# Column sums of the adaLN accumulators: matmuls with a column of ones, or transposes and row sums

## The chip, the cores and the metric

The kernel runs on one core of a Trainium2 chip. The metric is the device time of one execution in microseconds (us). Before the change the median of three runs is 1148.0 us (1146.42 to 1149.65).

## The reference

The program is a trunk of two layers over x (256 x 2048, f32) with a conditioning vector c of 2048 values. What the change touches is the modulation:

```python
cond = jax.nn.silu(c)
for i in range(DEPTH):
    mod = cond @ ada_w[i] + ada_b[i]
    shift, scale, gate = jnp.split(mod, 3, axis=-1)
    h = rms_norm(x, pre_g[i]) * (1 + scale[:, None, :]) + shift[:, None, :]
    ...
    y = sgu_mixer(h, ...) if i == 0 else mla_mixer(h, ...)
    x = x + gate[:, None, :] * rms_norm(y, post_g[i])
```

`ada_w[i]` is 2048 x 6144 f32, 50 MB per layer, and it is multiplied by a single vector. The mixer of layer 0 (SGU) projects h to 3 x 4096 columns (`u`, `v`, `z`), normalizes and mixes `v` along the sequence, multiplies, and projects back from 4096 to 2048. The mixer of layer 1 (MLA) projects h to 3072 columns (two latents, a rotary key, a gate `z`), expands the latents to 16 heads, attends, and projects back.

## The kernel before, in words

All large products run on PE with f32r operands that were split into a high and a low part; a product of two such numbers takes three matmuls. The weights come in **granules**: one load of 256 rows x 512 columns (512 KB) on SP's queue, a cast to the high part on ACT (line 113), and the difference to the low part on DVE (line 114). One granule feeds 12 matmuls of 128x512, since the 256 tokens are two blocks, each with two k-tiles and three products.

The class `Stream` sets the order of this work. `load` appends a transfer, `weights` a transfer with its stage of casting and subtracting, `hook` any other stage. When the matmuls of a granule are about to be written into the program, `get` runs stages until the one that is `AHEAD` + 1 = 5 granules further on is made (hooks on the way are run as they come), and `step` keeps the transfers `RAW_BUFS` = 6 loads ahead of the stages. The engines' programs are written in that order and each runs its own in order.

The modulation is too small for PE at full width, so it is done on DVE. `ada_items` makes one item per k-tile of 128 rows: a load into the same ring of raw buffers, and a hook that adds raw * silu(c)[k] to an accumulator `acc` of 128 x 1024 (line 294 for the first, 296 for the others). After 16 k-tiles the accumulator holds, for 1024 outputs, 128 partial sums each, one on each partition, which must be summed across the partitions, and the sums must lie on partitions as columns. `ada_sums` (line 305) does both with PE: for each 128 columns of the accumulator one matmul with a column of ones, eight for an accumulator of 1024, into one auxiliary bank (`aux_bank`, a ring of four PSUM banks that transposes and the SGU's mixing use as well). Its readers on DVE follow in the same hook: `ada_put` (lines 316 to 320) adds the bias to the shift and makes `amul`, `fin` of `ada_gate` (lines 347 and 349) makes `gcol`.

There are eight accumulators of 1024 from the middle of layer 0 on: two for layer 0's gate (`ada_gate(0)`, tiles `acc_gate`, `pgate`), four for layer 1's shift and scale (`ada_range(1, ...)`, tiles `acc_ada`, `pada`), two for layer 1's gate (`ada_gate(1)`). Layer 0's own shift and scale come before, in smaller ranges, and go through the same `ada_sums`.

The items are dealt out evenly among the granules by `spread`. The constants say how many: `E1` items of layer 0's gate go with the last part of the `u` and `v` projection, `E2` items with the `z` projection (`piz`), the rest with layer 0's output projection (`po`); of `gate1`, `G1` items go with layer 1's input projection (`pm`), the rest with the last output projection (`pp`). A gate half is 17 items, 16 accumulations and `fin`.

In layer 1 the two latents are normalized and turned while `pm_3` runs: `turn_latent` is called four times, a granule apart, with tiles `cqp`, `cqp`, `ckp`, `ckp`. Each takes an auxiliary bank, turns into it, and is read in the next granule by ACT (line 1058) and in the one after by DVE (line 1064), where the bank becomes free. `spread_gate` later turns `gcol` and broadcasts it along the rows through DRAM.

Of the kernel before, what the change touches and what calls it, by code (L numbers as in the profile page):

```python
# [12 lines left out]
AX = mybir.AxisListType  # L13
PSUM = bass.MemoryType.PSUM

P = 128
# [25 lines left out]
MUL = 3  # L42
AHEAD0 = 2
RAMP = 15
G1 = 23
E1 = 23
E2 = 32
LAG = 6
LAG1 = 7
PRE = 4  # L50
# [90 lines left out]
def spread(main, extra):  # L141

    if not main:
        return
    done = 0
    for i, m in enumerate(main):
        m()
        want = -(-len(extra) * (i + 1) // len(main))
        while done < want:
            extra[done]()  # L150
            done += 1
# [3 lines left out]
def tile_trunk(  # L155
# [7 lines left out]
    nc = tc.nc  # L163
    x = x[0]
    out = out[0]
# [10 lines left out]
    ST = Stream(nc, wp)  # L176
# [4 lines left out]
    def small(name, n):  # L181
        return sp.tile([P, n], F32, tag="sm", name=name, bufs=16)
# [4 lines left out]
    def aux_bank(name):  # L187
        return pa.tile([P, 512], F32, tag="ax", name=name)
# [15 lines left out]
    ident = const.tile([P, P], F32, name="ident")  # L204
# [72 lines left out]
    def ada_items(name, src, width, state):  # L277

        nk = 1024 // width
        todo = []  # L280
        for k in range(KD):
            def add(k=k):
                if k % nk == 0:
                    state["box"] = ST.raw_item(
                        f"{name}_{k}", nk, width,
                        [(lambda r, v=v: (r if v is None else r.rearrange("p k (t n) -> p k t n", t=2)[:, :, v, :]), a)
                         for v, a in src(k, nk)])

                def stage(box=state["box"]):
                    if k == 0:  # L290
                        state["acc"] = sp.tile([P, 1024], F32, tag="acc", name=f"acc_{name}", bufs=2)[:, 0:width]
                    acc, raw, w = state["acc"], box["raw"][:, k % nk, :], sc[:, k:k + 1]
                    if k == 0:
                        nc.vector.tensor_scalar_mul(acc, raw, w)
                    else:
                        nc.vector.scalar_tensor_tensor(acc, raw, w, acc, op0=ALU.mult, op1=ALU.add)  # L296

                ST.hook(stage)
            todo.append(add)
        return todo  # L300

    def ada_rows(l, k0, nk, c0, n):
        return ada_w[l, k0 * P:(k0 + nk) * P, c0:c0 + n].rearrange("(k p) n -> p k n", p=P)

    def ada_sums(name, n, state):
        ps = aux_bank(name)
        for j in range(n):
            nc.tensor.matmul(ps[:, j:j + 1], lhsT=state["acc"][:, j * P:(j + 1) * P], rhs=ones[:, 0:1],  # L308
                             start=True, stop=True)
        return ps  # L310

    def ada_put(l, k, n, ps_shift, ps_scale):

        ks = slice(k, k + n)
        i = l * 48 + k
        nc.vector.tensor_tensor(out=shift[:, l, ks], in0=ps_shift, in1=cols[:, 0, i:i + n], op=ALU.add)
        t = small(f"sc_{l}_{k}", n)
        nc.vector.tensor_tensor(out=t, in0=ps_scale, in1=cols[:, 0, i + 16:i + 16 + n], op=ALU.add)
        g = 96 + l * 16 + k
        nc.vector.scalar_tensor_tensor(amul[:, l, ks], t, 1.0, cols[:, 0, g:g + n], op0=ALU.add, op1=ALU.mult)  # L320

    def ada_cols(l, k0, nk, state):
        def fin():
            ps = ada_sums(f"pada_{l}_{k0}", 2 * nk, state)
            ada_put(l, k0, nk, ps[:, 0:nk], ps[:, nk:2 * nk])

        return fin

    def ada_range(l, k0, nk):

        st = {}
        n = nk * P
        return ada_items(
            f"ada_{l}_{k0}",
            lambda k, m: [(t, ada_rows(l, k, m, t * D + k0 * P, n)) for t in range(2)],
            2 * n, st) + [lambda: ST.hook(ada_cols(l, k0, nk, st))]

    def ada_gate(l):

        todo = []  # L340

        def fin(q, st):
            ps = ada_sums(f"pgate_{l}_{q}", 8, st)
            ks = slice(q * 8, q * 8 + 8)
            i = l * 48 + 32 + q * 8
            g = gcol[:, l, ks]
            nc.vector.tensor_tensor(out=g, in0=ps[:, 0:8], in1=cols[:, 0, i:i + 8], op=ALU.add)
            i = 40 + l * 16 + q * 8
            nc.vector.tensor_tensor(out=g, in0=g, in1=cols[:, 1, i:i + 8], op=ALU.mult)

        for q in range(2):
            st = {}
            c0 = 2 * D + q * 1024
            todo += ada_items(f"gate_{l}_{q}", lambda k, m, c0=c0: [(None, ada_rows(l, k, m, c0, 1024))], 1024, st)
            todo.append(lambda q=q, st=st: ST.hook(lambda: fin(q, st)))
        return todo

# [75 lines left out]
    turned = {}  # L433
# [56 lines left out]
    def w_chunk(name, w, k0, nk, n, slots=()):  # L490
        return [lambda k=k: ST.weights(f"{name}_{k}", w[k * P:min(k + 2, k0 + nk) * P, n * 512:(n + 1) * 512],
                                       slot=slot if k in slots else None)
                for k in range(k0, k0 + nk, 2)]
# [6 lines left out]
    while cells < 256:  # L500
        have = sum(nk for k0, nk, at in STEPS if at <= cells)
        n = min(order, key=lambda n: (got[n], n))
        if have == KD:
            n = [m for m in list(range(8, 16)) + list(range(8)) if got[m] < KD][0]
        if got[n] == have:
            n = max(order, key=lambda n: have - got[n])
# [61 lines left out]
    for k in range(KD):  # L568
# [6 lines left out]
        if k == WAT:  # L575
            n = visits[0][0]
# [24 lines left out]
    todo = []  # L601
    si = 1
    ada1 = [f for k0 in range(0, KD, 4) for f in ada_range(1, k0, 4)]
    for n, k0, nk, at in visits:
        while si < len(STEPS) and at >= STEPS[si][2]:
# [3 lines left out]
            todo = []  # L609
            si += 1  # L610
        todo += w_chunk(f"wi_{n}_{k0}", sgu_w_in, k0, nk, n) if at else []
    extra = ada_gate(0) + ada1
    spread(todo, extra[:E1])
    spread([f for n in range(16, 24) for f in w_chunk(f"wi_{n}", sgu_w_in, 0, KD, n)], extra[E1:E1 + E2])

    xr = [[None] * 4 for _ in range(NB)]

    def load_xr(b, q):
# [3 lines left out]
    spread([f for n in range(4) for f in w_chunk(f"wo_{n}", sgu_w_out, 0, 32, n)],  # L622
            extra[E1 + E2:] + [lambda b=b, q=q: ST.load(lambda: load_xr(b, q)) for b in range(NB) for q in range(4)])
    gate1 = ada_gate(1)
    spread(w_chunk("wm_0", mla_w_in, 0, KD, 0, WSLOTS), [])
    spread([f for n in range(1, 5) for f in w_chunk(f"wm_{n}", mla_w_in, 0, KD, n)], gate1[:G1])
    QK = NOPE + ROPE
# [21 lines left out]
    for p in range(8):  # L649
        todo = []  # L650
# [6 lines left out]
    spread(rest_o[:3], [])  # L657
    spread(rest_o[3:] + w_chunk("wp_2", mla_w_out, 0, KD, 2), gate1[G1:])
    spread(w_chunk("wp_3", mla_w_out, 0, KD, 3), [])
# [115 lines left out]
    for j, (n, k0, nk, _) in enumerate(rest):  # L775
        t = visit(n, k0, nk)
# [36 lines left out]
    for j in range(8):  # L813
        t = chunk_tasks(f"piz_{j}", range(KD), lhs0, ev_z(j))
# [93 lines left out]
    for n in range(4):  # L908
        t = chunk_tasks(f"po_{n}", range(32), lhs_y, ev_out(0, n, ready1))
# [61 lines left out]
    t = chunk_tasks("pm_0", range(KD), lhs1, ev_lat(0))  # L971
# [121 lines left out]
    t = chunk_tasks("pm_2", range(KD), lhs1, ev_sz(0))  # L1093
# [5 lines left out]
    t = chunk_tasks("pm_3", range(KD), lhs1, ev_sz(1))  # L1099
# [245 lines left out]
    t = chunk_tasks("pp_2", range(KD), lhs_o, ev_out(1, 2, finish))  # L1345
# [3 lines left out]
    t = chunk_tasks("pp_3", range(KD), lhs_o, ev_out(1, 3, finish))  # L1349
# [51 lines left out]
```

## Time and profile before

| | |
|---|---|
| median of 3 runs | 1148.0 us (1146.42 to 1149.65) |
| the profiled execution | 1147.47 us |
| its span in the profile | 1145.7 us |
| PE busy (matmuls) | 1120.1 us, 98% |
| DVE busy | 892.8 us, 78% |
| ACT busy | 567.6 us, 50% |
| mean of the DMA | 266 GB/s |

The span is what lies between the first and the last instruction of the profiled execution; 1.8 us of its time lie outside. Matmuls are pipelined: each lasts longer than the distance to the next one's start, so the records of PE overlap and a cost on PE is read from starts or from the chain of waits, not from durations. In the chain a piece is a run of work of one kind that, followed back from the last instruction, was each time what released the next.

### The profile page before, as it was taken

How to read it: one execution, taken by the hardware profiler on the slowest of the kernel's cores; microseconds unless marked ns; L12 is line 12 of the kernel's file. 1: busy time of each engine (PE TensorE's matmuls, PEld its weight loads, DVE VectorE, ACT ScalarE, POOL GpSimd, SP SyncE). 2: the span in 40 equal slices, each digit the busy share in tenths (PEclk: the TensorE clock that was granted, in tenths of full speed). 3: DMA queues.
4: the chain of work that ended last, by engine and by line, in shares of the span. 5: the costliest groups of instructions: out<-in, count | busy, mean ns of one | idle time of the engine just before them, and what ended most of it. 6: DMA issues, size and time to landing. Idle time of an engine off the chain costs nothing.

```text
span 1145.7 us, 15806 instructions
## 1 busy us (share of the span) xinstructions
PE 1120.1 (98%) x5681; PEld 953.2 (83%) x5681; DVE 892.8 (78%) x1187; ACT 567.6 (50%) x813; POOL 23.9 (2%) x51
## 2 busy tenths in 40 slices
PE   5999999999999999999999999999999999999997
PEld 5788878888888888888888888888888999999885
DVE  4889898978987887888787878757878467568755
ACT  3665434354545655555444434447574445455441
POOL 1000000000000000000001000000000000000000
PEclk9999999999999999999999999999999999999999
DMA  9999898978887987788689989972988445345672
GB/s 321 321 325 323 267 359 302 362 274 271 294 287 228 307 272 244 258 269 293 227 301 350 377 324 351 364 252 86 369 287 277 147 158 167 92 148 188 228 271 85
DMA packets 158207, 304.35 MB, mean 266 GB/s; under 512 B 12057, under 2 KB 29056, under 8 KB 158128
## 3 DMA queue, kind: packets, MB, share of 16 engines
q1 hardware_dynamic: 156128, 297.84, 75.9%
q0 software_dynamic: 1968, 5.49, 1.7%
q8 instruction: 45, 0.74, 0.3%
q14 instruction: 34, 0.28, 0.1%
q10 hardware_dynamic: 32, 0.01, 0.0%
HBM read 301.17 MB, written 2.11 MB: 265 GB/s over the span
## 4 chain that ended last, share of the span: by engine, by line
PE 86%; DMA 5%; DVE 4%; ACT 2%; issue 2%; SPq 0%; DVEq 0%; ACTq 0%
PE pi L191 23%; PE piz L191 15%; PE po L191 15%; PE pm L191 10%; PE pp L191 8%; DMA wi<-in_sgu_w_in_dram 2%; PE k L191 2%; PE v L191 2%; PE s L191 2%; PE qn L191 2%; DMA ada<-in_ada_w_dram 1%; PE o L191 1%; PE pada L308 1%; PE mix L191 1%; DMA first<-in_ada_w_dram 1%
## 5 line engine op out<-in xcount | busy, mean ns | idle before, releaser
L296 DVE SCALAR_TENSOR_TENSOR acc_ada<-ada,sc,acc_ada 128x1024 f32<-128x1024 f32 (+1 forms) x135 | 148.6, 1101 | 0.9
L296 DVE SCALAR_TENSOR_TENSOR acc_gate<-gate,sc,acc_gate 128x1024 f32<-128x1024 f32 x60 | 76.6, 1277 | 0.0
L676 DVE TENSOR_TENSOR part<-pi,part 128x512 f32<-128x512 f32 x92 | 59.6, 683 | 4.8 <-PE pi L191 4.7
L113 ACT CAST wi_6h<-wi 128x1024 fp32r<-128x1024 f32 x24 | 25.1, 1051 | 40.3 <-DMA wi<-in_sgu_w_in_dram 32.0
L113 ACT CAST wi_8h<-wi 128x1024 fp32r<-128x1024 f32 x24 | 25.2, 1049 | 28.1 <-DMA wi<-in_sgu_w_in_dram 20.1
L113 ACT CAST wi_4h<-wi 128x1024 fp32r<-128x1024 f32 x24 | 25.2, 1051 | 26.7 <-DMA wi<-in_sgu_w_in_dram 26.0
L114 DVE TENSOR_TENSOR wi_10l<-wi,wi_10h 128x1024 fp32r<-128x1024 f32 x24 | 29.3, 1220 | 6.8 <-ACT wi_10h L113 6.8
L114 DVE TENSOR_TENSOR wi_12l<-wi,wi_12h 128x1024 fp32r<-128x1024 f32 x24 | 29.2, 1217 | 5.3 <-ACT wi_12h L113 5.1
L114 DVE TENSOR_TENSOR wi_14l<-wi,wi_14h 128x1024 fp32r<-128x1024 f32 x24 | 29.3, 1221 | 4.6 <-ACT wi_14h L113 4.6
L114 DVE TENSOR_TENSOR wi_6l<-wi,wi_6h 128x1024 fp32r<-128x1024 f32 x24 | 29.2, 1219 | 4.6 <-ACT wi_6h L113 4.6
L114 DVE TENSOR_TENSOR wi_8l<-wi,wi_8h 128x1024 fp32r<-128x1024 f32 x24 | 29.3, 1219 | 3.4 <-ACT wi_8h L113 3.4
L113 ACT CAST wi_2h<-wi 128x1024 fp32r<-128x1024 f32 x24 | 25.2, 1052 | 13.3 <-DMA wi<-in_sgu_w_in_dram 13.0
L114 DVE TENSOR_TENSOR wi_4l<-wi,wi_4h 128x1024 fp32r<-128x1024 f32 x24 | 29.3, 1219 | 2.7 <-ACT wi_4h L113 2.7
L114 DVE TENSOR_TENSOR wi_0l<-wi,wi_0h 128x1024 fp32r<-128x1024 f32 x23 | 28.1, 1222 | 3.6 <-ACT wi_0h L113 3.4
L1245 ACT ACTIVATE sm<-sm,nm 128x128 f32<-128x128 f32 (+1 forms) x32 | 14.3, 448 | 32.6 <-DVE nm L1243 32.6
L114 DVE TENSOR_TENSOR wi_2l<-wi,wi_2h 128x1024 fp32r<-128x1024 f32 x24 | 29.3, 1220 | 1.3 <-ACT wi_2h L113 1.3
L113 ACT CAST wi_0h<-wi 128x1024 fp32r<-128x1024 f32 x23 | 24.0, 1051 | 12.5 <-DMA wi<-in_sgu_w_in_dram 12.5
L113 ACT CAST wi_10h<-wi 128x1024 fp32r<-128x1024 f32 x24 | 25.1, 1045 | 9.9 <-DMA wi<-in_sgu_w_in_dram 9.2
L113 ACT CAST wi_14h<-wi 128x1024 fp32r<-128x1024 f32 x24 | 25.1, 1045 | 5.5 <-PE pi L191 4.0
L113 ACT CAST wi_12h<-wi 128x1024 fp32r<-128x1024 f32 x24 | 25.2, 1049 | 5.3 <-PE pi L191 3.6
L191 PE MATMUL pi<-wi_4h,hH 128*128 128x512 f32 x64 | 25.3, 396 | 1.2 <-DVE part L676 1.2
L770 DVE SCALAR_TENSOR_TENSOR part<-mix,cols,part 128x256 f32<-128x256 f32 x32 | 13.3, 477 | 16.3 <-PE mix L191 16.3
(690 smaller groups left out, 3816.1 us busy)
## 6 DMA issues: line engine op xcount, KB each, us to landing
wi<-in_sgu_w_in_dram SPq DMA_DIRECT2D x191, 512.0 KB, 5.4
ada<-in_ada_w_dram SPq DMA_DIRECT2D x240, 256.0 KB, 5.2
gate<-in_ada_w_dram SPq DMA_DIRECT2D x64, 512.0 KB, 5.0
wo<-in_sgu_w_out_dram SPq DMA_DIRECT2D x64, 512.0 KB, 6.3
wm<-in_mla_w_in_dram SPq DMA_DIRECT2D x48, 512.0 KB, 5.2
wp<-in_mla_w_out_dram SPq DMA_DIRECT2D x32, 512.0 KB, 4.9
ukv<-in_mla_w_ukv_dram SPq DMA_DIRECT2D x16, 512.0 KB, 4.7
uq<-in_mla_w_uq_dram SPq DMA_DIRECT2D x12, 384.0 KB, 3.2
```

The source lines that it names most:

```text
L113: self.nc.scalar.copy(out=h, in_=raw)
L114: self.nc.vector.tensor_tensor(out=l[0:rows], in0=raw[0:rows], in1=h[0:rows].bitcast(F32), op=ALU.subtract)
L191: nc.tensor.matmul(o, lhsT=l, rhs=r, start=start, stop=stop)
L296: nc.vector.scalar_tensor_tensor(acc, raw, w, acc, op0=ALU.mult, op1=ALU.add)
L308: nc.tensor.matmul(ps[:, j:j + 1], lhsT=state["acc"][:, j * P:(j + 1) * P], rhs=ones[:, 0:1], start=True, stop=True)
L676: nc.vector.tensor_tensor(out=part[n, b], in0=ps, in1=part[n, b], op=ALU.add)
L770: nc.vector.scalar_tensor_tensor(u[:, cs], ps[:, cs], bs_col(2 * j + i), u[:, cs], op0=ALU.add, op1=ALU.mult)
L1245: nc.scalar.activation(sm[:, i, :], sm[:, i, :], AF.Exp, bias=nm[:, i:i + 1], scale=scale, accum_out=su[:, i:i + 1])
```

## The change

The eight large accumulators are no longer summed by `ada_sums`. A new hook, `ada_turn`, turns each accumulator with eight transposes against the identity into two auxiliary banks of 128 x 512, four tiles in each. A second new hook, `ada_rowsums`, lets DVE sum the rows of both banks (`reduce_sum` over the last axis of a 128 x 4 x 128 view, once per bank) into a small tile of eight columns in SBUF, from which `ada_put` or `fin` reads as before. The two are separate items of the stream, so that other work can stand between them, and `G1`, `E1` and `E2` grow from 23, 23 and 32 to 24, 24 and 34. Layer 0's own ranges still go through `ada_sums`.

```diff
--- before.py
+++ after.py
@@ -42,9 +42,9 @@
 MUL = 3
 AHEAD0 = 2
 RAMP = 15
-G1 = 23
-E1 = 23
-E2 = 32
+G1 = 24
+E1 = 24
+E2 = 34
 LAG = 6
 LAG1 = 7
 PRE = 4
@@ -309,6 +309,22 @@
                              start=True, stop=True)
         return ps
 
+    def ada_turn(name, n, state):
+
+        state["turned"] = []
+        for i in range(0, n, 4):
+            ps = aux_bank(f"{name}_{i}")
+            for j in range(4):
+                nc.tensor.transpose(out=ps[:, j * P:(j + 1) * P], in_=state["acc"][:, (i + j) * P:(i + j + 1) * P],
+                                    identity=ident)
+            state["turned"].append((i, ps))
+
+    def ada_rowsums(name, n, state):
+        t = small(name, n)
+        for i, ps in state.pop("turned"):
+            nc.vector.reduce_sum(out=t[:, i:i + 4], in_=ps.rearrange("p (j q) -> p j q", q=P), axis=AX.X)
+        return t
+
     def ada_put(l, k, n, ps_shift, ps_scale):
 
         ks = slice(k, k + n)
@@ -321,7 +337,7 @@
 
     def ada_cols(l, k0, nk, state):
         def fin():
-            ps = ada_sums(f"pada_{l}_{k0}", 2 * nk, state)
+            ps = (ada_sums if l == 0 else ada_rowsums)(f"pada_{l}_{k0}", 2 * nk, state)
             ada_put(l, k0, nk, ps[:, 0:nk], ps[:, nk:2 * nk])
 
         return fin
@@ -333,14 +349,15 @@
         return ada_items(
             f"ada_{l}_{k0}",
             lambda k, m: [(t, ada_rows(l, k, m, t * D + k0 * P, n)) for t in range(2)],
-            2 * n, st) + [lambda: ST.hook(ada_cols(l, k0, nk, st))]
+            2 * n, st) + ([lambda: ST.hook(lambda: ada_turn(f"tada_{l}_{k0}", 2 * nk, st))] if l else []) + [
+                lambda: ST.hook(ada_cols(l, k0, nk, st))]
 
     def ada_gate(l):
 
         todo = []
 
         def fin(q, st):
-            ps = ada_sums(f"pgate_{l}_{q}", 8, st)
+            ps = ada_rowsums(f"pgate_{l}_{q}", 8, st)
             ks = slice(q * 8, q * 8 + 8)
             i = l * 48 + 32 + q * 8
             g = gcol[:, l, ks]
@@ -352,6 +369,7 @@
             st = {}
             c0 = 2 * D + q * 1024
             todo += ada_items(f"gate_{l}_{q}", lambda k, m, c0=c0: [(None, ada_rows(l, k, m, c0, 1024))], 1024, st)
+            todo.append(lambda q=q, st=st: ST.hook(lambda: ada_turn(f"tgate_{l}_{q}", 8, st)))
             todo.append(lambda q=q, st=st: ST.hook(lambda: fin(q, st)))
         return todo
```

How the instructions stand on the engines is shown at two places. In the names the number behind the last underscore is a buffer's.

The first is the latent stage, where the first half of layer 1's gate (`acc_gate_0`) is summed while `pm_3` runs. On PE, before: the last two transposes of the first `ckp`, the sums, and the next granule's matmuls; in brackets the engines whose semaphores an instruction waits for.

```order
L1053 MATMUL ckp_7482<-ident,kvn_7213 128x128
L1053 MATMUL ckp_7482<-ident,kvn_7265 128x128
L308 MATMUL pgate_0_7489<-ones,acc_gate_0_6961 128x1 [waits DVE_49]
L308 MATMUL pgate_0_7489<-ones,acc_gate_0_6961 128x1 x7
L191 MATMUL pm_0_7409<-wm_6h,h1H_1_6697 128x512 [waits Activation_49]
L191 MATMUL pm_0_7409<-wm_6h,h1L_1_6715 128x512
```

The sums stood behind the first `ckp`, which waited for nothing of its own.

PE now: the last two transposes of the second `cqp`, then the turned accumulator.

```order
L1071 MATMUL cqp_7477<-ident,qn_7234 128x128
L1071 MATMUL cqp_7477<-ident,qn_7286 128x128
L318 MATMUL tgate_0_0_7484<-ident,acc_gate_0_6985 128x128 [waits DVE_49]
L318 MATMUL tgate_0_0_7484<-ident,acc_gate_0_6985 128x128 x3
L318 MATMUL tgate_0_4_7489<-ident,acc_gate_0_6985 128x128 x4
L191 MATMUL pm_0_7433<-wm_4h,h1H_1_6721 128x512 [waits Activation_49]
L191 MATMUL pm_0_7433<-wm_4h,h1L_1_6739 128x512
```

The block moved up by a granule of `pm_3` and now stands in front of the first `ckp`, which gained a wait for DVE and PE:

```order
L191 MATMUL pm_1_7440<-wm_4h,h1H_1_6899 128x512
L191 MATMUL pm_1_7440<-wm_4h,h1L_1_6908 128x512
L191 MATMUL pm_1_7440<-wm_4l,h1H_1_6899 128x512
L1071 MATMUL ckp_7516<-ident,kvn_7237 128x128 [waits DVE_49,PE_49]
L1071 MATMUL ckp_7516<-ident,kvn_7289 128x128
```

Before, that stood at the second `ckp` alone. On DVE in the same place, before:

```order
L114 TENSOR_TENSOR wm_10l<-wm_10_7357,wm_10h 128x1024
L114 TENSOR_TENSOR wm_12l<-wm_12_7375,wm_12h 128x1024
L1064 SCALAR_TENSOR_TENSOR cql_7425<-cqp_7423,cols,cqh_7424 128x256 x2
L347 TENSOR_TENSOR gcol<-pgate_0_7489,cols 128x8
L349 TENSOR_TENSOR gcol<-gcol,cols 128x8
L114 TENSOR_TENSOR wm_14l<-wm_14_7378,wm_14h 128x1024
L1064 SCALAR_TENSOR_TENSOR cql_7455<-cqp_7453,cols,cqh_7454 128x256
L1064 SCALAR_TENSOR_TENSOR cqh_7454<-cqp_7453,cols,cqh_7454 64x256
```

`gcol` stood between the reads of the two `cqp`.

and now:

```order
L114 TENSOR_TENSOR wm_12l<-wm_12_7384,wm_12h 128x1024
L1082 SCALAR_TENSOR_TENSOR cql_7449<-cqp_7447,cols,cqh_7448 128x256 x2
L325 TENSOR_REDUCE pgate_0_7523<-tgate_0_0_7484 128x4
L325 TENSOR_REDUCE pgate_0_7523<-tgate_0_4_7489 128x4
L364 TENSOR_TENSOR gcol<-pgate_0_7523,cols 128x8
L366 TENSOR_TENSOR gcol<-gcol,cols 128x8
L114 TENSOR_TENSOR wm_14l<-wm_14_7402,wm_14h 128x1024
L1082 SCALAR_TENSOR_TENSOR cql_7479<-cqp_7477,cols,cqh_7478 128x256
L1082 SCALAR_TENSOR_TENSOR cqh_7478<-cqp_7477,cols,cqh_7478 64x256
```

The row sums moved in ahead of `gcol`, between the read of the first `cqp` and those of the second; the rest of these rows kept its order.

The second place is the second half of layer 0's gate (`acc_gate_1`) on DVE, in the `z` projection. Before:

```order
L114 TENSOR_TENSOR wi_2l<-wi_2_3676,wi_2h 128x1024
L753 TENSOR_TENSOR vl_1_3797<-part_1_614,vh_1_3774 128x512
L114 TENSOR_TENSOR wi_4l<-wi_4_3713,wi_4h 128x1024
L770 SCALAR_TENSOR_TENSOR part_0_373<-mix_0_3830,cols,part_0_373 128x256 x2
L770 SCALAR_TENSOR_TENSOR part_1_375<-mix_1_3839,cols,part_1_375 128x256 x2
L296 SCALAR_TENSOR_TENSOR acc_gate_1_3086<-gate_1_15_3733,sc,acc_gate_1_3086 128x1024
L114 TENSOR_TENSOR wi_6l<-wi_6_3736,wi_6h 128x1024
L114 TENSOR_TENSOR wi_8l<-wi_8_3766,wi_8h 128x1024
L797 TENSOR_TENSOR part_0_344<-part_0_344,z_0_3878 128x512
L797 TENSOR_TENSOR part_1_346<-part_1_346,z_1_3881 128x512
L347 TENSOR_TENSOR gcol<-pgate_1_3898,cols 128x8
L349 TENSOR_TENSOR gcol<-gcol,cols 128x8
```

The last accumulation came behind the reads of `mix`, four instructions ahead of `gcol`.

and now:

```order
L296 SCALAR_TENSOR_TENSOR acc_gate_1_3090<-gate_1_15_3680,sc,acc_gate_1_3090 128x1024
L114 TENSOR_TENSOR wi_2l<-wi_2_3717,wi_2h 128x1024
L771 TENSOR_TENSOR vl_1_3805<-part_1_614,vh_1_3781 128x512
L114 TENSOR_TENSOR wi_4l<-wi_4_3720,wi_4h 128x1024
L788 SCALAR_TENSOR_TENSOR part_0_373<-mix_0_3837,cols,part_0_373 128x256 x2
L788 SCALAR_TENSOR_TENSOR part_1_375<-mix_1_3846,cols,part_1_375 128x256 x2
L114 TENSOR_TENSOR wi_6l<-wi_6_3740,wi_6h 128x1024
L114 TENSOR_TENSOR wi_8l<-wi_8_3770,wi_8h 128x1024
L815 TENSOR_TENSOR part_0_344<-part_0_344,z_0_3892 128x512
L815 TENSOR_TENSOR part_1_346<-part_1_346,z_1_3895 128x512
L325 TENSOR_REDUCE pgate_1_3912<-tgate_1_0_3855 128x4
L325 TENSOR_REDUCE pgate_1_3912<-tgate_1_4_3860 128x4
```

The last accumulation stands ahead of the split of `wi_2` instead of behind the reads of `mix`. On PE the transposes stand there two granules (24 matmuls) ahead of where the sums stood. Of the eight blocks, both halves of layer 0's gate and the first of layer 1 stand two granules earlier, the fourth of layer 1 and both halves of layer 1's gate one granule, and the second and third of layer 1 where the sums stood.

## Rows read from the trace of the kernel before

**Rows 1.** The page: busy us by engine, share; granted clock by slice.

```profile
PE 1120.1 (98%) x5681; PEld 953.2 (83%) x5681; DVE 892.8 (78%) x1187; ACT 567.6 (50%) x813; POOL 23.9 (2%) x51
...
PEclk9999999999999999999999999999999999999999
```

**Rows 2.** Stretches: us, busy us by engine, granted clock, DMA share, GB/s.

```profile
600.00:770.00 170.00, 170.00 (x780) 141.53 (x779) 130.15 (x130) 73.15 (x88) 3.40 (x6) 1.00 0.96 343
```

**Rows 3.** The chain that ended last: start us, us, what.

```profile
252.00 97.94 PE pi L191 x432
349.93 1.68 PE pgate L308 x16
...
681.91 54.57 PE po L191 x240
...
1102.80 1.68 PE pgate L308 x16
```

**Rows 4.** The same chain, from 425 to 460 us.

```profile
428.61 0.87 PE yt L808 x8
429.48 5.46 PE piz L191 x24
...
450.48 1.68 PE pgate L308 x16
```

**Rows 5.** Line 308, column sums: count, ns min/median/max, first and last start.

```profile
L308 PE MATMUL pada<-ones,acc_ada x120: 164/250/250, 53.9 to 737.9; 128*128 128x1 f32 x120
...
L308 PE MATMUL pgate<-ones,acc_gate x64: 164/250/250, 349.8 to 1104.2; 128*128 128x1 f32 x64
```

**Rows 6.** Tile yt: transposes on PE and their reader on DVE.

```profile
L808 PE MATMUL yt<-ident,part x64: 270/272/273, 428.4 to 601.8; 128*128 128x128 f32 x64
...
L197 DVE TENSOR_TENSOR yL<-yt,yH x16: 680/687/693, 429.7 to 602.9; 128x512 fp32r<-128x512 f32 x16
```

**Rows 7.** Waits: who for whom, us in total, times, longest.

```profile
DVE shift L316 <- PE pada L308: 11.7, 7, 4.0
...
DVE gcol L347 <- PE pgate L308: 8.0, 4, 4.3
...
PE pada L308 <- DVE acc_ada L296: 0.4, 1, 0.4
```

**Rows 8.** DVE in order of time, near the first gate block.

```profile
349.50 1.28 DVE L676 TENSOR_TENSOR part<-pi,part 128x512 f32<-128x512 f32 x2
```

**Rows 9.** Tile acc_gate: the accumulations of the gates on DVE.

```profile
L296 DVE SCALAR_TENSOR_TENSOR acc_gate<-gate,sc,acc_gate x60: 1272/1277/1283, 266.3 to 1097.6; 128x1024 f32<-128x1024 f32 x60
L294 DVE TENSOR_SCALAR acc_gate<-gate,sc x4: 742/745/753, 261.1 to 863.8; 128x1024 f32<-128x1024 f32 x4
```

**Rows 10.** PE in order of time, in the latent stage.

```profile
859.00 0.60 PE L1053 MATMUL ckp<-ident,kvn 128*128 128x128 f32 x4
859.44 1.84 PE L308 MATMUL pgate<-ones,acc_gate 128*128 128x1 f32 x16
861.14 0.48 PE L191 MATMUL pm<-wm_6h,h1H 128*128 128x512 f32 x1
...
863.98 0.60 PE L1053 MATMUL ckp<-ident,kvn 128*128 128x128 f32 x4
```

**Rows 11.** DVE in order of time, in the latent stage.

```profile
853.98 1.28 DVE L296 SCALAR_TENSOR_TENSOR acc_gate<-gate,sc,acc_gate 128x1024 f32<-128x1024 f32 x1
...
859.14 0.87 DVE L1064 SCALAR_TENSOR_TENSOR cql<-cqp,cols,cqh 128x256 fp32r<-128x256 f32 x2
861.32 0.17 DVE L347 TENSOR_TENSOR gcol<-pgate,cols 128x8 f32<-128x8 f32 x1 [1.31 <-PE pgate L308]
...
863.24 0.49 DVE L1064 SCALAR_TENSOR_TENSOR cqh<-cqp,cols,cqh 64x256 fp32r<-64x256 f32 x1
```

**Rows 12.** DVE in order of time, before the second gate block.

```profile
440.05 1.22 DVE L114 TENSOR_TENSOR wi_2l<-wi,wi_2h 128x1024 fp32r<-128x1024 f32 x1
...
445.91 1.27 DVE L296 SCALAR_TENSOR_TENSOR acc_gate<-gate,sc,acc_gate 128x1024 f32<-128x1024 f32 x1
```

## The prediction

> **What bounds the kernel now.** I read the page first, then the stretches, then the chain of waits in order of time, and only then single lines. The page gives PE 98% of a span of 1145.7 us and DVE 78%, and the granted clock is full in every slice [rows 1]. A high share alone does not make PE the bound, so the stretch in which the DMA engines are busiest is read next: from 600 to 770 us the transfers take 0.96 of the engines' time and PE is still busy for 170.00 us of 170 [rows 2]. The chain says the same from the other side: from 252 us to the last matmuls nearly all of it is pieces of PE. Its longest, 432 matmuls in 97.94 us, sets the pace of one matmul at 97.94 / 432 = 0.2267 us [rows 3]. In this chain stand eight pieces that the change takes out, the column sums of the four gate accumulators and of layer 1's four, 1.68 us each, the first at 349.93, the last at 1102.80 [rows 3, 4]. They lie on the path that sets the end; whatever they shrink by, everything behind them moves forward by, as long as nothing else becomes late.
>
> **Removed: 64 column sums.** Each block has eight matmuls of one column, and the trace counts 64 records for the 32 sums of the gates, two passes per sum [rows 5]. A block's price is its piece of 1.68 us and what it does to the matmuls after it: the 240 that follow one at 681.91 take 54.57 us where 240 x 0.2267 = 54.41, so 0.16 more [rows 3]. That is 1.84 us for a block, 0.115 us a pass. The block at 859.44 stands behind four transposes, and the next ordinary matmul starts 1.70 us after it [rows 10]; I take 1.70 there. Removed: 7 x 1.84 + 1.70 = 14.6 us.
>
> **Added: 64 transposes.** The kernel already transposes 128x128 f32 tiles against the same identity. For `yt` the trace has 64 records for 64 transposes, one pass each [rows 6], and in the chain eight of them are a piece of 0.87 us, the 24 matmuls behind it taking 5.46 where 24 x 0.2267 = 5.44 [rows 4]. So a block of eight costs 0.89 us, 0.111 each: a pass costs what it cost before, and there are half as many. Seven blocks gain 1.84 - 0.89 = 0.95 each, 6.65 together; the eighth, where the transposes join four others, 1.70 - 0.87 = 0.83.
>
> The row that speaks against this is the duration of one transpose, 272 ns [rows 6]: matmuls overlap, so I count the distance from start to start and not the duration. The Trainium skill (TensorE: Matmul & The Clock Gate, Part 4: PE-mode transpose) gives about 275 ns for a 128x128 transpose inside a kernel; as an estimate from that page, 64 x 0.275 = 17.6 us would replace 14.6, a loss of 3.0 where I count a gain of 7.5. For a block of eight the trace disagrees with that page by a factor of 2.5.
>
> **Added: 16 row sums on DVE.** No row shows a reduction of 128x4x128. The nearest is a DVE operation that reads 128x512 f32 from PSUM: 0.687 us alone [rows 6], and two behind each other in 1.28 [rows 8]; I take 0.64 us. Below, half of a 1024 wide single-source operation, 0.37; above, a whole 1024 wide accumulation, 1.28 [rows 9]. That is 10.2 us of DVE, between 5.9 and 20.5. What it displaces is idle time: DVE stood 8.0 us waiting for the gates' sums and up to 11.7 for the others [rows 7], because sums and reader were issued together. Now the transposes are issued one or two granules (12 matmuls, 2.72 us each) before their reader in six of the eight blocks, and in the other two DVE has a weight split to do in between, so the waits go and the row sums take their place. I price DVE at nothing on the path, save at one place.
>
> **That place is the latent stage, near 859 us.** There are four auxiliary PSUM banks, used in turn. A block took one and now takes two, so the first `ckp` reuses the bank of the first `cqp`, and the second `ckp` that of the second; before, only the second `ckp` had to wait, and for the first `cqp`. In times of the profile before [rows 10, 11]: PE comes to the first `ckp` at 859.00 + 0.87 = 859.87, DVE's two reads of the first `cqp` run from 859.14 for 0.87, to 860.01: PE waits 0.14. It comes to the second 863.98 - 859.00 - 1.70 = 3.28 later, at 863.29. DVE starts its two row sums at 860.01 instead of standing until 861.32, ends them at 861.29, and from there goes on as before, so the last read of the second `cqp` ends at 863.24 + 0.49 = 863.7: PE waits 0.4. Together 0.55, with the bounds of the row sum 0.2 to 1.9. This block gains 0.83 - 0.55 = 0.3.
>
> **Moved: the accumulations and their loads.** The transposes stand up to two granules earlier than the sums did, and must not meet an unfinished accumulator. The last accumulation of the second gate block ended at 445.91 + 1.27 = 447.18 [rows 12], and the transposes would want it 5.44 us before 450.48, at 445.04. But the new counts move it too: it now stands ahead of the split that began at 440.05, so it ends near 441.3, 3.7 us in time. The tightest is the block in the latent stage, whose last accumulation does not move: it ended at 853.98 + 1.28 = 855.26 [rows 11], and the transposes come when the second `cqp` is done, 2.72 and 0.13 before 859.00, so at 856.15, 0.9 in time. SP's loads of `gate` and `ada` move forward past one weight load each; each stretch keeps its number of loads (the 23 items of the first carried 16 + 6, and so do the 24 now, the one more being a hook), so no queue carries more bytes. PE's one wait for an accumulator so far was 0.4 us [rows 7].
>
> **Sum.** 6.65 + 0.3 = 7.0 us (5.6 with the longest row sum, 7.5 without any bank wait). The profiled execution took 1147.47 us, so 1140.5; the median of the three runs, 1148.0, lies 0.5 above it, and would give 1141.0. I say 1140.8.
>
> **Rivals.**
>
> *Part of the gain is given back by new waits.* PE would wait at blocks whose accumulations do not in fact come earlier, because their loads land no sooner. For: the DMA engines at 0.96 [rows 2]. Price: 2.1 us at the second gate block as above; the same again at the first block of layer 1, which also moves two granules, would make 4.2, so 1140.8 + 4.2 = 1145.0. Against: their loads are issued sooner too, by the same queue, and the code lets it run six loads ahead of the stage that uses them.
>
> *No gain.* If this transpose ran in two passes as the sums do, a block would cost its 1.84 again, and with the 0.55 of the latent stage the time would be 1148.0. Against: one record per transpose for `yt` [rows 6].
>
> *Slower, by the transposes' length.* If blocks of eight ran at 0.272 us each, 64 x 0.272 = 17.4 against 14.6, with the 0.55 a loss of 3.4: 1150.9. It decides from 0.115 x 2 = 0.23 us a transpose on. Against: 0.87 for eight in the same chain [rows 4]. The Trainium skill (the same page and part) would have it so.
>
> **How the numbers follow.** The forecast has 0.80. New waits get 0.10, half of it beyond 0.3%, which is 3.4 us here and about the least that a measurement of this kernel can tell from no change. No gain has 0.05. Slower has 0.05, of which 0.03 beyond the 0.3%, since 3.4 us is just that bound. So faster 0.80 + 0.05 = 0.85; same 0.05 + 0.05 + 0.02 = 0.12; slower 0.03. The range: from 7.5 gained, 1140.0, less the 1.6 by which the fastest of the runs before lies under their median, so 1138.4, up to the rival of new waits, 1145.0.
>
> **What would show it.** Right: PE has 64 records fewer; in the chain the eight pieces are transposes of about 0.87; DVE's waits for `pgate` and for layer 1's `pada` are gone, and its busy time is about 903; the row sums last 0.6 to 0.7; a wait of PE for DVE of about half a microsecond in the latent stage and nowhere else. The first block of transposes stands near 344.3, and each ordinary matmul behind a block is about 0.95 us more ahead than behind the block before. Wrong: eight transposes take more than 1.2 us, PE waits for `acc_gate` or `acc_ada` over 1 us at several blocks, or the gain is there at 860 and lost behind it.

## The result and the profile after

The changed kernel takes 1141.65 us in the median of four runs (1141.42 to 1141.84), the kernel before 1148.3 (four runs, one more than above); the ratio is 0.9949, 95% interval 0.9937 to 0.9961. In five later runs its median was 1142.99 (1141.96 to 1143.22), the ratio 0.9959 [0.9945, 0.9972]. So it is faster, by 4.8 to 6.7 us. The profiled execution took 1141.84 us against 1147.47: 5.6 us where the sum said 7.0.

The page of the changed kernel: span, then busy us of each engine, share, instructions.

```profile
span 1140.1 us, 15692 instructions
...
PE 1114.2 (98%) x5617; PEld 945.7 (83%) x5617; DVE 901.7 (79%) x1203; ACT 566.6 (50%) x813; POOL 23.8 (2%) x51
```

Against [rows 1], PE has 64 records fewer and is busy 5.9 us less, DVE has 16 instructions more and is busy 8.9 us longer. The chain has transposes where the sums stood [rows 3, 4]. The chain of the changed kernel from 443 to 460 us: start us, us, what.

```profile
445.44 0.87 PE tgate L318 x8
446.31 8.21 PE piz L191 x36
```

The six blocks outside the latent stage that stand in the chain all read 0.87. The first, at 344.2, does not stand in it, since the chain of this kernel can be followed back only to 387 us; in PE's timeline the next matmul starts 0.79 us after it. The tile tgate of the changed kernel: count, ns min/median/max, first and last start.

```profile
L318 PE MATMUL tgate<-ident,acc_gate x32: 270/273/273, 344.2 to 1095.9; 128*128 128x128 f32 x32
L325 DVE TENSOR_REDUCE pgate<-tgate x8: 675/678/684, 354.5 to 1097.1; 128x4 f32<-128x512 f32 x8
```

One record a transpose, as for `yt` [rows 6], and a row sum of 0.68 us. What the page does not say is where 1.4 us of the gain stayed. The waits of PE in the changed kernel do: us in total, times, longest.

```profile
PE pi L191 <- DVE part L694: 2.2, 3, 1.2
...
PE ckp L1071 <- DVE cql L1082: 0.2, 1, 0.2
...
PE piz L191 <- DVE part L694: 0.2, 1, 0.2
```

The same list of the kernel before has no `ckp` or `piz` in it, and two waits for `part`:

```profile
PE pi L191 <- DVE part L676: 1.6, 2, 1.2
```

Two waits are new outside the latent stage. PE of the changed kernel in order of time:

```profile
354.13 0.47 PE L191 MATMUL pi<-wi_12h,hH 128*128 128x512 f32 x1 [0.69 <-DVE part L694]
...
398.58 0.47 PE L191 MATMUL piz<-wi_0h,hH 128*128 128x512 f32 x1 [0.16 <-DVE part L694]
```

To price them I compare the start of the same ordinary matmul in the two timelines. Ahead of 300 us executions differ by up to 1.7 us where the order is the same (at 300 us the kernel with every row sum twice, whose order is the changed kernel's up to 344 us, stood 1.4 us behind the kernel before, and a second execution of the changed kernel 0.3 us ahead of it), so all sums below start there. The change of the offset to the kernel before, in us, negative where a kernel gains (the columns are the changed kernel and the experiments that follow):

| Stretch | changed | e1_23 | sums_new_counts | two_pass | no_rowsums | ahead | twice_rowsums |
|---|---|---|---|---|---|---|---|
| first gate block, 344 to 352 | -0.92 | -0.92 | 0.00 | -0.02 | -0.90 | -0.90 | -0.90 |
| 352 to 365 | +0.98 | +0.01 | +0.05 | +0.03 | +0.98 | 0.00 | +2.06 |
| 365 to 399 | +0.41 | +0.01 | +0.44 | +0.46 | +0.42 | +1.88 | +0.74 |
| five blocks, 440 to 745 | -4.69 | -4.71 | +0.03 | -0.19 | -4.69 | -4.70 | -4.69 |
| latent stage, 850 to 866 | -0.53 | -0.90 | 0.00 | +0.04 | -0.61 | -0.20 | +0.12 |
| last block, 900 to 1106 | -0.91 | -0.92 | -0.06 | -0.04 | -0.90 | -0.91 | -0.92 |
| 300 to 1106, all in all | -5.55 | -7.34 | +0.59 | +0.39 | -5.53 | -4.65 | -3.46 |

Each block brings what was forecast, 0.91 to 0.94. But the first block's gain is gone 10 us behind it, and 0.41 us more is lost near 398.

### The profile page after: what moved, and what is told of

The parts are those of the page before. It is cut to its first block, busy times and chain, and to the rows that moved or that the text cites. A ratio compares the mean times of both kernels' runs of the same rounds, so it can differ in the third digit from the quotient of the medians.

```text
span 1140.1 us, 15692 instructions
## 1 busy us (share of the span) xinstructions
PE 1114.2 (98%) x5617; PEld 945.7 (83%) x5617; DVE 901.7 (79%) x1203; ACT 566.6 (50%) x813; POOL 23.8 (2%) x51
## 4 chain that ended last, share of the span: by engine, by line
PE 59%; DVE 3%; ACT 2%; DMA 1%; issue 0%; DVEq 0%; ACTq 0%
PE piz L191 15%; PE po L191 15%; PE pm L191 8%; PE pp L191 8%; PE k L191 2%; PE v L191 2%; PE s L191 2%; PE qn L191 2%; PE o L191 1%; PE mix L191 1%; DMA wm<-in_mla_w_in_dram 1%; PE qr L191 1%; PE yt L826 1%; DMA wi<-in_sgu_w_in_dram 0%; DVE acc_gate L296 0%
## 5 line engine op out<-in xcount | busy, mean ns | idle before, releaser
L114 DVE TENSOR_TENSOR wi_10l<-wi,wi_10h 128x1024 fp32r<-128x1024 f32 x24 | 29.3, 1219 | 12.5 <-ACT wi_10h L113 12.3
L113 ACT CAST wi_2h<-wi 128x1024 fp32r<-128x1024 f32 x24 | 25.2, 1050 | 12.8 <-DMA wi<-in_sgu_w_in_dram 12.3
L707 ACT ACTIVATE part<-part 128x512 f32<-128x512 f32 x16 | 9.9, 633 | 35.5 <-DVE part L694 35.5
```

Of the source, the lines that this page charges most:

```text
L113: self.nc.scalar.copy(out=h, in_=raw)
L114: self.nc.vector.tensor_tensor(out=l[0:rows], in0=raw[0:rows], in1=h[0:rows].bitcast(F32), op=ALU.subtract)
L707: nc.scalar.activation(part[n, b], part[n, b], AF.Gelu)
```

## Experiments

Two theories on that loss. **A: the new counts.** E1 = 24 puts the gates' accumulations in other places among the weight splits, DVE is late with the splits, and PE meets that at 354 and 398. **B: the row sums.** They are new work of DVE, 1.28 us a block, and PE waits for them.

### The counts back, the transposes kept (e1_23)

```diff
-E1 = 24
-E2 = 34
+E1 = 23
+E2 = 35
```

> The changed kernel with E1 and E2 set so that layer 0's ranges take one item fewer per step in the first stretch (E1 = 23 as before the change, E2 = 35 to carry the rest). Theory A (the gates' accumulations, moved ahead of the weight splits by E1 = 24, make the splits late on DVE, and PE loses 0.88 us at 354 and 0.48 us at 398 for that): the 0.69 us wait of PE for DVE's part after the first gate block goes, the profiled time is 0.9 to 1.4 us under the changed kernel's, about 1140.4, the median about 1140.5. Theory B (the row sums themselves, 1.28 us of DVE each block, make the splits late): the wait stays behind the block wherever it stands, and the time is the changed kernel's, 1141.6.

Measured: 1140.56 us (1140.41 to 1142.6, five runs), ratio 0.9938 [0.9924, 0.9952]; profiled 1140.87. Both waits are gone, and the kernel gains 7.34 us from 300 on against 5.55. So 1.39 us of the loss come from the order that the counts set, and B's expectation fell; another 0.37 lie in the latent stage, which differs from one execution to the next (below). E1 also moves the first block of transposes: it stands at 350.48 here and at 344.21 in the changed kernel. That the waits went for this reason is ruled out further below, by a kernel whose block stands earlier still and whose wait at 354 is gone all the same.

How the order does it is in DVE's timeline. The changed kernel, with idle time and its cause in brackets:

```profile
276.41 0.69 DVE L694 TENSOR_TENSOR part<-pi,part 128x512 f32<-128x512 f32 x1 [0.67 <-PE pi L191]
278.73 1.23 DVE L114 TENSOR_TENSOR wi_10l<-wi,wi_10h 128x1024 fp32r<-128x1024 f32 x1 [1.64 <-ACT wi_10h L113]
279.88 1.28 DVE L712 BATCH_NORM_STATS2 stats<-part 128x6 f32<-128x512 f32 x2
281.07 1.27 DVE L296 SCALAR_TENSOR_TENSOR acc_gate<-gate,sc,acc_gate 128x1024 f32<-128x1024 f32 x1
```

The same with E1 = 23:

```profile
277.23 0.69 DVE L694 TENSOR_TENSOR part<-pi,part 128x512 f32<-128x512 f32 x1 [0.67 <-PE pi L191]
277.84 1.27 DVE L296 SCALAR_TENSOR_TENSOR acc_gate<-gate,sc,acc_gate 128x1024 f32<-128x1024 f32 x1
279.57 1.23 DVE L114 TENSOR_TENSOR wi_10l<-wi,wi_10h 128x1024 fp32r<-128x1024 f32 x1 [0.45 <-ACT wi_10h L113]
280.71 1.28 DVE L712 BATCH_NORM_STATS2 stats<-part 128x6 f32<-128x512 f32 x2
```

ACT of the changed kernel in the same place:

```profile
277.13 0.63 ACT L707 ACTIVATE part<-part 128x512 f32<-128x512 f32 x1 [0.73 <-DVE part L694]
277.67 1.03 ACT L113 CAST wi_10h<-wi 128x1024 fp32r<-128x1024 f32 x1
```

After two `part` operations DVE has nothing to do until ACT has read `part` and then made the high half of the next weight; ACT waits for no load in between. With E1 = 23 the accumulation stands in that hole, and DVE idles 0.45 us behind it. With E1 = 24 it stands one place later, DVE idles 1.64 us and does the accumulation afterwards: 1.2 us of DVE lost. Six waits of 1.64 us stand in DVE's timeline between 278 and 327. DVE's waits from 250 to 345 us, first of the changed kernel:

```profile
DVE wi_10l L114 <- ACT wi_10h L113: 12.3, 6, 4.1
```

and with E1 = 23, as in the kernel before (6.4 there too):

```profile
DVE wi_10l L114 <- ACT wi_10h L113: 6.4, 6, 4.1
```

What it comes to: from the split of `wi_10` at 257.51 to that of `wi_8` at 352.15 DVE of the changed kernel takes 94.6 us; with E1 = 23 the same 93 instructions take 90.7 us (258.33 to 349.07). DVE is 3.9 us late there against E1 = 23, and no row sum has run by then; the first starts at 354.50.

### The counts without the transposes (sums_new_counts)

```diff
-            ps = ada_rowsums(f"pgate_{l}_{q}", 8, st)
+            ps = ada_sums(f"pgate_{l}_{q}", 8, st)
...
-            todo.append(lambda q=q, st=st: ST.hook(lambda: ada_turn(f"tgate_{l}_{q}", 8, st)))
+            todo.append(lambda: ST.hook(lambda: None))
```

(and the same for layer 1)

> The new counts (E1 = 24, E2 = 34, G1 = 24) and the extra hook, which does nothing here, with the matmul sums of the kernel before: no transposes, no row sums. Theory A (the counts move accumulations ahead of splits and cost 0.9 to 1.4 us): slower than the kernel before by 0.9 to 1.4 us, about 1149.4, and PE's waits for DVE's part near 354 are there without any row sum. Theory B (the row sums cost it): the kernel before's time within 0.4 us, 1148.0. A third possibility, that the counts alone gain (accumulations that come sooner), would give less than 1147.5.

Measured: 1148.08 us (11 runs), ratio 1.0003 [0.9994, 1.0011]. A's number, 1149.4, was wrong here, and the time is the one that B gave; B falls by the other runs. The loss at 398 is there without any row sum (+0.44), but nothing is lost at 354. The splits are as late as in the changed kernel (that of `wi_8` starts at 352.17 here and at 352.15 there); a block of 1.84 us hides it, one of 0.89 does not. The kernel of the next experiment, with the long block where the changed kernel has the short one, loses nothing at 354 either. So at 354 the two halves of the change meet: the shorter block only uncovers a DVE that the counts have made late.

### An ordinary matmul in place of each transpose (two_pass)

```diff
-                nc.tensor.transpose(out=ps[:, j * P:(j + 1) * P], in_=state["acc"][:, (i + j) * P:(i + j + 1) * P],
-                                    identity=ident)
+                mm(ps[:, j * P:(j + 1) * P], state["acc"][:, (i + j) * P:(i + j + 1) * P], ident, True, True)
```

> The changed kernel with an ordinary matmul against the identity in place of each transpose; the result is the same turned tile. If a block's price is its number of passes (one per transpose, two per f32 matmul, 0.111 to 0.115 us each), the trace has 64 records more than the changed kernel, each block is 0.95 us dearer, the pieces of the chain are 1.7 again, and the time is 1141.6 + 7 x 0.95 + 0.83 = 1149.1, less up to 0.9 if the wait at 354 is covered by the longer block: 1148.2 to 1149.1. If the price is something else (the one column against 128, the change of stationary operand), the time stays within 1 us of 1141.6.

Measured: 1147.78 us (11 runs), ratio 0.9996 [0.9987, 1.0005]: the whole gain is gone, and the time is 0.4 us under the least that was expected. The tile tgate of this kernel, and behind it its chain:

```profile
L191 PE MATMUL tgate<-ident,acc_gate x64: 270/275/275, 344.2 to 1101.9; 128*128 128x128 f32 x64
```

```profile
445.41 1.79 PE tgate L191 x16
```

Two records each, and blocks of 1.78 to 1.79 us against 1.68 for the one-column sums [rows 3, 4]. A pass costs 0.105 us with one column and 0.112 with 128. The number of passes sets the price, as the prediction had it.

### No row sums, and each row sum twice (no_rowsums, twice_rowsums)

The first kernel leaves the sums along the rows out and copies four columns instead.

```diff
-            nc.vector.reduce_sum(out=t[:, i:i + 4], in_=ps.rearrange("p (j q) -> p j q", q=P), axis=AX.X)
+            nc.vector.tensor_copy(out=t[:, i:i + 4], in_=ps[:, 0:4])
```

> The changed kernel with each row sum on DVE replaced by a copy of four columns of the turned tile: the summing along rows is left out. Theory A (the counts cost the 1.3 us at 354 and 398): the time falls by the latent stage's wait alone, 0.3 to 0.5 us, to about 1141.2; the 0.69 us wait at 354 stays. Theory B (the row sums cost it): the time falls by 1.3 to 1.8 us, to about 1140.1, and the wait at 354 is gone.

Measured: 1142.06 us (1141.79 to 1143.46), ratio 0.9950 [0.9937, 0.9963], the changed kernel's time. The losses at 354 and 398 stay to 0.01 us. B is out.

```diff
-            nc.vector.reduce_sum(out=t[:, i:i + 4], in_=ps.rearrange("p (j q) -> p j q", q=P), axis=AX.X)
+            for _ in range(2):
+                nc.vector.reduce_sum(out=t[:, i:i + 4], in_=ps.rearrange("p (j q) -> p j q", q=P), axis=AX.X)
```

> The changed kernel with every row sum run twice, 16 x 0.68 = 10.9 us more of DVE. If DVE's row sums are covered everywhere but in the latent stage: PE waits there up to 1.3 us longer at the two ckp, and the time is 1141.6 to 1142.9. If they take PE's time one for one at each block: 8 x 1.3 = 10.4 us, 1152. If they caused the losses at 354 and 398: the waits there grow by 1.3 us each, 1144.2.

Measured: 1143.19 us (1143.16 to 1145.44), ratio 0.9965 [0.9953, 0.9977], between the first and the third of the times expected. The five blocks from 440 to 745 gain the same 4.69: there DVE has at least 1.28 us of slack at every block. At the first block it has none beyond the one row sum. PE of this kernel:

```profile
355.73 0.47 PE L191 MATMUL pi<-wi_12h,hH 128*128 128x512 f32 x1 [0.73 <-DVE part L695]
...
362.25 0.47 PE L191 MATMUL pi<-wi_8h,hH 128*128 128x512 f32 x1 [0.80 <-DVE part L695]
```

The first wait is the changed kernel's; the second is new, and with it 1.1 us are lost up to 365 and 0.3 more near 398. Why one row sum was free there shows beside the kernel with the new counts and the old sums. DVE in the changed kernel:

```profile
354.50 1.28 DVE L325 TENSOR_REDUCE pgate<-tgate 128x4 f32<-128x512 f32 x2
...
356.21 1.23 DVE L114 TENSOR_TENSOR wi_10l<-wi,wi_10h 128x1024 fp32r<-128x1024 f32 x1
```

and with the old sums:

```profile
354.51 0.16 DVE L347 TENSOR_TENSOR gcol<-pgate,cols 128x8 f32<-128x8 f32 x1
...
356.23 1.23 DVE L114 TENSOR_TENSOR wi_10l<-wi,wi_10h 128x1024 fp32r<-128x1024 f32 x1 [1.36 <-ACT wi_10h L113]
```

The split starts at the same time: the two row sums fill a wait for ACT of 1.36 us. It is the hole of the first experiment again.

### The same counts, each accumulation one split earlier (ahead)

```diff
-def spread(main, extra):
+def spread(main, extra, ahead=False):
...
-        m()
+        if not ahead:
+            m()
...
+        if ahead:
+            m()
...
-    spread(todo, extra[:E1])
+    spread(todo, extra[:E1], True)
```

By the wording of A, accumulations further ahead of the splits should cost more; by the hole, less.

> The changed kernel with the same counts (E1 = 24, E2 = 34), but in the first stretch each accumulation is issued ahead of the weight load and split that it followed, so one split earlier. Theory A1 (accumulations that stand ahead of splits make the splits late, the further ahead the later): the splits before 345 are at least as late as in the changed kernel, the wait at 354 is 0.7 us or more, 1141.6 or slower. Theory A2 (an accumulation costs nothing where DVE waits for ACT's high part anyway, between the two part operations and the split, and 1.2 us where it stands behind that split; the changed counts moved six of them behind it): the order is part, part, accumulation, split again, DVE's wait for ACT's wi_10h between 250 and 345 falls from 12.3 us to about 6.4, the wait at 354 goes, and the time falls by up to 0.9 us, to about 1140.8; the 0.5 us at 398 may stay, since in the second stretch the accumulations stand behind the splits here.

Measured: 1142.57 us (1142.37 to 1143.09), ratio 0.9956 [0.9944, 0.9969]. A2 holds at its place: DVE's wait for `wi_10h` from 250 to 345 falls from 12.3 to 6.1 us, the wait at 354 is gone, and from 300 to 365 the kernel gains 0.96 us more than the changed one. The first block of transposes of e1_23 and of this kernel:

```profile
350.48 1.04 PE L318 MATMUL tgate<-ident,acc_gate 128*128 128x128 f32 x8
```

```profile
341.14 1.03 PE L321 MATMUL tgate<-ident,acc_gate 128*128 128x128 f32 x8
```

So the wait goes with the short block later than in the changed kernel and with the short block earlier: it is the splits and not the place of the block. The time did not fall, though: accumulations behind 345 us now miss the holes. DVE waits longer for the same splits; first the changed kernel, then this one:

```profile
377.30 1.22 DVE L114 TENSOR_TENSOR wi_14l<-wi,wi_14h 128x1024 fp32r<-128x1024 f32 x1 [1.15 <-ACT wi_14h L113]
```

```profile
376.25 1.23 DVE L114 TENSOR_TENSOR wi_14l<-wi,wi_14h 128x1024 fp32r<-128x1024 f32 x1 [2.35 <-ACT wi_14h L113]
```

PE pays for nearly all of it at one matmul:

```profile
398.74 0.47 PE L194 MATMUL piz<-wi_0h,hH 128*128 128x512 f32 x1 [1.31 <-DVE part L697]
```

### The changed kernel and e1_23 once more

> The changed kernel once more, unaltered, beside the others on one chip: 1141.6 within 0.3 us, and the two losses at 354 (0.7 us wait) and at 398 in the same places. If they stand elsewhere, they are no property of the order.

Measured: 1142.99 us as told above; the waits stand at the same matmuls (0.8 us at 354, 0.2 at 398). The kernel's own time spreads more than expected, the losses do not move.

> The changed kernel with E1 = 23 and E2 = 35 once more, since the executions of one kernel spread over 1 us or more. By the first run 1140.6, against 1141.6 to 1143.0 of the changed kernel; the waits at 354 and 398 are absent. If its median is 1141.6 or more, the 1.1 us that the first run showed was chance.

Measured: 1140.51 us (1139.9 to 1141.19), ratio 0.9936 [0.9922, 0.9950]; no wait at 354 or 398. The `ckp` wait in the latent stage, absent in the first profile of this kernel, is 0.5 us in this one, and the gain from 300 on is 6.67 us.

### Layer 0 turned as well, and the latent block moved

With E1 = 23 there is DVE time for more of the same. Layer 0's later ranges have blocks of eight sums at 176 and 240 us.

```diff
-            ps = (ada_sums if l == 0 else ada_rowsums)(f"pada_{l}_{k0}", 2 * nk, state)
+            if l == 0:
+                ada_turn(f"tada_{l}_{k0}", 2 * nk, state)
+            ps = ada_rowsums(f"pada_{l}_{k0}", 2 * nk, state)
```

> The changed kernel with E1 = 23 and E2 = 35, and with layer 0's five ranges behind the first turned by transposes and summed along rows as well (the transposes and row sums in the one hook that had the matmul sums, no item more). If the price of a block lies on the path there too: the two blocks of eight near 176 and 240 gain 0.95 us each, the three of four before 100 us gain nothing (PE waits for loads there), so 1.9 us under the kernel with E1 = 23 alone, 1138.7. If DVE sets the pace there (it is busy 0.89 of 185 to 345 us, PE waits 1.2 to 1.7 us for it near 165), the row sums, 7 x 0.64 us, take the place of the gain: 1140.6, or up to 1.3 us more.

Measured: 1139.14 us (1138.25 to 1140.35), ratio 0.9925 [0.9913, 0.9938]. The matmuls behind 300 us stand 1.9 us further ahead than those at 172, as worked out.

The wait of PE for `cql` in the latent stage was left. Two kernels move the block by G1 = 21 and G1 = 22 on top of this one.

> The kernel with layer 0 turned as well (E1 = 23, E2 = 35), and G1 = 21, which moves the transposes of the block in the latent stage behind the four pkr transposes, so that both ckp find their banks free. If the wait of PE for DVE's cql there (0.4 us in that kernel's profile) comes from the bank that the block takes: it goes, and nothing waits in its place, 0.3 to 0.4 us under that kernel: 1138.8. If DVE is simply late in that stage, the wait moves to pkr or to the next projection: 1139.1 as before.

> The same with G1 = 22: the block stands between the second ckp and pkr. If the bank is the cause, ckp no longer waits, but pkr takes the bank after the block's and may wait for DVE's reads of the first or second ckp instead: 1138.8 to 1139.1. If DVE is simply late, 1139.1.

Measured: G1 = 21 takes 1138.11 us (1137.41 to 1138.77), ratio 0.9916 [0.9902, 0.9930]; G1 = 22 takes 1137.23 (1137.17 to 1137.82), ratio 0.9909 [0.9895, 0.9923]. In both `ckp` no longer waits, and the latent stage gains 0.6 us more than with G1 = 24; the rest of the difference to 1139.14 lies ahead of 172 us and is not G1's. With G1 = 21 PE waits 0.2 us for the accumulator of the last block and loses 0.3 us there, which I had not expected. PE with G1 = 22:

```profile
850.58 0.60 PE L1073 MATMUL ckp<-ident,kvn 128*128 128x128 f32 x4
...
853.79 0.60 PE L1073 MATMUL ckp<-ident,kvn 128*128 128x128 f32 x4
854.22 1.04 PE L318 MATMUL tgate<-ident,acc_gate 128*128 128x128 f32 x8
```

This kernel, E1 = 23, E2 = 35, G1 = 22 and all of layer 0's ranges but the first turned, is the fastest of the study, some 10 us under the kernel before.

## Why the prediction was right, and where it was not

**Removed and added: right.** A block went from 1.84 to 0.89: the five blocks from 440 to 745 gained 4.69 together, 0.94 each, where 0.95 was said. The transposes follow each other at 0.87 / 8 = 0.109 us. The Trainium skill (TensorE: Matmul & The Clock Gate, Part 4: PE-mode transpose) gives about 275 ns for one in a kernel; the trace has that as the duration of a record, 273 ns, but the distance from one to the next is what a block costs. Both rivals on this step fell: no block rose to 1.2 us. Had the transposes run in two passes, the gain would have gone: two_pass shows it, at 1147.78 where the rival said 1148.0.

**Row sums: right.** 0.68 us each and 1.28 for two, DVE 901.7 us busy where 903 was said. Priced at nothing, they cost nothing: leaving them out changed the sum by 0.02 us. The waits of DVE for `pgate` and layer 1's `pada` [rows 7] are gone.

**Latent stage: the size about right, the parts not.** The net gain was said to be 0.3; it was 0.53 in the first profile and 0.31 in the second. The first `ckp` waits as described, 0.18 and 0.4 us (0.14 said). The second was to wait 0.4 for the row sums and waits for nothing. DVE and PE of the changed kernel:

```profile
854.99 0.87 DVE L1082 SCALAR_TENSOR_TENSOR cql<-cqp,cols,cqh 128x256 fp32r<-128x256 f32 x2
855.78 1.27 DVE L325 TENSOR_REDUCE pgate<-tgate 128x4 f32<-128x512 f32 x2
...
859.01 0.49 DVE L1082 SCALAR_TENSOR_TENSOR cqh<-cqp,cols,cqh 64x256 fp32r<-64x256 f32 x1
```

```profile
856.01 0.63 PE L1071 MATMUL ckp<-ident,kvn 128*128 128x128 f32 x4 [0.18 <-DVE cql L1082]
...
859.23 0.60 PE L1071 MATMUL ckp<-ident,kvn 128*128 128x128 f32 x4
```

The second `ckp` starts at 859.23 while the last read of the second `cqp` runs to 859.50, so it does not need that read to be over, and my account of the bank that it takes was wrong. With every row sum twice it is plainer still; PE and DVE of that kernel:

```profile
862.86 0.60 PE L1072 MATMUL ckp<-ident,kvn 128*128 128x128 f32 x4
```

```profile
863.60 0.48 DVE L1083 SCALAR_TENSOR_TENSOR cql<-cqp,cols,cqh 128x256 fp32r<-128x256 f32 x1
```

The second `ckp` is over there before DVE begins to read the second `cqp`. Which bank it takes is not shown. The wait that is there stands ahead of the row sums, and without them the stage gained only 0.08 us more (no_rowsums, -0.61). What lets the first `ckp` wait more or less is open: in the two profiles of E1 = 23 the stage gained 0.90 and 0.25 us with one order, so that 0.3 comes near is in part luck.

**Moved accumulations: the step that failed.** The prediction asked of the new counts only whether the accumulators would be ready for the transposes; they were, PE waits for none of them. It did not ask what their new place does to the splits on DVE, and it said that PE would wait for DVE in the latent stage "and nowhere else". The runs show in its place a DVE that is 3.9 us late at 352, from accumulations that stand behind its waits for ACT instead of in them, of which PE paid 0.98 at 354, where only the longer block had hidden it, and 0.41 at 398, where DVE is still 3.7 us late against E1 = 23. With those counts undone, the sum from 300 on is 7.34 and, in the second profile, 6.67, against the 7.0 said.

**The rival of new waits** came in part, 1.4 us of its 4.2, but by another way: no PE wait for an accumulation of the eight blocks appeared, and at the six holes ACT waits for no load. Near 398 the chain of the changed kernel does go over a load of `wi` (5.48 us, to 394.6), so that loads add to the 0.41 there is not excluded.

**The median.** The sum said 1140.5 for the profiled execution, which took 1141.84: the 1.4 us above. It said 1140.8 for the median; the runs gave 1141.65 and 1142.99. The second is 1.3 us higher with the same waits at the same matmuls in its profiled execution, which itself took 1141.96. Where the other four of those runs lost time is not recorded; in the traces at hand, executions of code in the same order differ by that much ahead of 172 us.

## What to carry to other kernels

When two engines make a weight in turns, the waits of the second for the first are free places: an operation that stands in one costs nothing, the same operation one place later cost the second engine 1.2 of its 1.27 us here. The engine that sets the end pays only for what is late when it gets there, 1.4 us here. So whoever changes how many items are spread over a stretch moves all of them in or out of these places, and should read the order around every such wait, not only the due times. And a shorter block on the critical engine pays only while its feeders are early: look at what the longer block was hiding.

## What the runs showed of the hardware that I had not expected

An f32 matmul against 128 columns costs nearly the same as one against a single column: 1.79 us for 16 passes against 1.68. And instructions in the same order reached 172 us with a spread of 1.7 us between executions, which is as large as the loss that this study was after. What sets it was not traced; in the kernel before, the chain goes over loads up to 166 us. Only the comparison of the same matmul in two timelines told them apart.
